# Paged attention in steps of four pages, keys and values fetched apart, and the prompt bias added by TensorE

## The chip, the cores and the metric

One NeuronCore of a Trainium2 chip runs the whole program. The metric is the device time of one execution in microseconds. Three runs of the kernel before took 2260.86, 2262.31 and 2270.95 us; the median is 2262.31 us.

## What is computed

One inference step of a decoder with two layers, for a prompt of 512 tokens and for eight samples of four tokens each that share the weights. Each layer projects the residual stream into four head groups: a short gated convolution (A), gated DeltaNet (B), HGRN2 (C) and differential attention with a relative bias (D). Their outputs are concatenated and projected back, followed by a layer norm, a channel mixer (a SwiGLU in layer 0, eight experts in layer 1) and another layer norm. The change is in group D alone:

```python
def _diff_attn_core(q, k, v, q_pos, k_pos, lam, rel_bias):
    s = jnp.einsum('bqhmd,bkhmd->bmhqk', q, k) * (HEAD_DIM_DQK ** -0.5)
    bias = jnp.transpose(rel_bias[_t5_bucket(q_pos, k_pos)], (2, 0, 1))
    s = jnp.where(k_pos[None, :] <= q_pos[:, None], s + bias, -jnp.inf)
    p = jax.nn.softmax(s, axis=-1)
    w = p[:, 0] - lam * p[:, 1]
    return jnp.einsum('bhqk,bkhv->bqhv', w, v)
```

There are 4 heads, each with two maps (m) of width 32 and values of width 64. The prompt attends to itself in blocks of 128 queries. Each sample attends to 2048 past positions, held in 16 pages of 128 positions that a page table names, and to its own four new tokens.

## The kernel before

All engines are programmed through a framework that takes the instructions in program order, finds their dependences tile by tile, and plans each engine's queue ahead of time from estimated durations: an instruction earlier in the program has priority when it is ready in the plan, and later ones fill what is left. On the chip every engine then works through its own queue in that fixed order. So the instructions of one stage lie between those of others.

`mixers` (line 477) holds the four head groups of a layer. In program order it runs `d_in` (the projections of D), `mix_b`, `d_attn`, `mix_a`, `mix_c` and the gates. `mix_b` has a long serial chain of small VectorE work with four round trips through DRAM; the attention of D and the projections of A and C (the tile `st`, split in three fp32r products of 128 by 128 weights) fill around it.

`d_sample` (line 596) does the samples in two groups g of four samples b. A step j takes one page of each of the four samples. `page` (line 607) reads page numbers into registers of SyncE, eight at a time, and issues one fetch of 256 KB for each page: 128 partitions of 2 KB, of which the first half is the transposed keys and the second half the values. The buffer `kv` has KVB = 9 slots of 2 KB a partition, shared with the exponentials of the prompt heads. Then, for each step:

- eight products of the queries `qs` with the keys: 32 columns of weights, 128 moving columns, sample b writing PSUM partitions 32b to 32b + 31. The loop is over the two tiles tl outside and over b inside (line 626). In the trace this is `dx<-kv,qs`.
- reduce_max on VectorE (L632), exp on ScalarE (L634), one transposition on TensorE (L635), its copy by VectorE (L637).
- four products with the values, 256 moving columns (`dx<-kv,et`), and `select` (lines 600 to 603), which keeps each row's own head with a multiplication and a reduction on VectorE.

16 steps, and one for the new tokens, make a group; then the 17 partial results are weighted and added (lines 658 to 674).

`d_head` (line 676) is one block of 128 queries of one prompt head, 16 in a layer. For both maps it multiplies queries and keys over nk = 128 to 512 positions (`dx<-arr,y`), adds the bias of the last 256 positions on VectorE in PSUM (L691), takes the maximum (L692) and the exponential (L694). VectorE then scales the second map (L699) and joins the two (L700); TensorE transposes the result into a third PSUM tile (L703) and multiplies by the values. `d_attn` runs a head after every second step.

An fp32 product is two passes on TensorE, and the trace has two records for it; a product of fp32r operands, and a transposition, is one.

Of the kernel before, what the change touches and what calls it, by code (L numbers as in the profile page):

```python
# [18 lines left out]
L = 2  # L19
# [20 lines left out]
KVB = 9  # L40
# [146 lines left out]
def _pack(a):  # L187
# [19 lines left out]
    f["kv"] = _cols(np.concatenate([kp, a["cache_v"].reshape(L, npool, 128, 256)], 3))  # L207
# [58 lines left out]
def _body(ctx, tc, I, O):  # L266
# [210 lines left out]
    def mixers(l, y32, hook):  # L477
# [110 lines left out]
        def d_attn(q, k, vt, qs):  # L588
            heads = [d_head(q, k, vt, qb, tl, h2) for qb in range(4) for tl in range(2) for h2 in range(2)]
            for n, _ in enumerate(d_sample(k, vt, qs)):  # L590
                if n % 2 == 1:
                    heads[n // 2]()
            for i in range(2):
                rms_d(y32[:, 6:8], i, nd[:, l:l + 1])

        def d_sample(k, vt, qs):
            od = y32[:, 6:8]
            ends = []

            def select(pj, po):  # L600
# [4 lines left out]
            regs = []  # L605

            def page(i):
                if i == len(regs):
                    with ExitStack() as qx:
                        if len(ends) > 8:  # L610
                            qx.enter_context(tc.issue_after(ends[-9].ins))
                        _, r = nc.values_load_multi_w_load_instructions(ptb[:, i:i + 8], engines=[mybir.EngineType.SP],
                                                                        min_val=0, max_val=I["kv"].shape[1] - 1)
                    regs.extend(r)
                t = dq.tile([128, 512], F32, name="kv", bufs=KVB)
                ends.append(SP.dma_start(t, I["kv"][l][bass.ds(regs[i], 1)].rearrange("o p f -> p (o f)")))
                return t

            for g in range(2):
                nm = dq.tile([128, 20], F32, name="nm", bufs=2)  # L620
                zz = dq.tile([128, 20], F32, name="zz", bufs=2)
                pj = dq.tile([128, 17, 64], F32, name="pj", bufs=1)
                for j in range(16):
                    kv = [page(64 * g + 4 * j + b) for b in range(4)]
# [5 lines left out]
                    if j == 15:  # L630
                        tt(V, ps[:, 0:128], ps[:, 0:128], bs[:, 0:128], OP.add)
                    V.reduce_max(nm[:, j:j + 1], ps[:, 0:128], axis=AX.X, negate=True)  # L632
                    e = dq.tile([128, 128], F32, name="e", bufs=3)
                    S.activation(e, ps[:, 0:128], AF.Exp, bias=nm[:, j:j + 1], accum_out=zz[:, j:j + 1])  # L634
                    PE.transpose(ps[:, 128:256], e, ident)  # L635
                    et = dq.tile([128, 128], F32, name="et", bufs=3)
                    V.tensor_copy(et, ps[:, 128:256])  # L637
                    for b in range(4):
                        mm(ps[32 * b:32 * b + 32, 256:512], et[:, 32 * b:32 * b + 32], kv[b][:, 256:512])
                    select(pj[:, j], ps[:, 256:512])  # L640
# [6 lines left out]
                V.reduce_max(nm[:, 16:17], ps[:, 0:32], axis=AX.X, negate=True)  # L647
                sn = dq.tile([128, 32], F32, name="sn", bufs=1)
                S.activation(sn, ps[:, 0:32], AF.Exp, bias=nm[:, 16:17], accum_out=zz[:, 16:17])
                pe = dx()  # L650
                PE.transpose(pe[0:32, 0:128], sn, ident)
                etn = dq.tile([32, 128], F32, name="etn", bufs=1)
                V.tensor_copy(etn, pe[0:32, 0:128])
                po = dx()
                for b in range(4):
                    mm(po[32 * b:32 * b + 32, 0:256], etn[:, 32 * b:32 * b + 32], vt[0:32, 4, :])
                select(pj[:, 16], po[:, 0:256])
                V.tensor_reduce(nm[:, 17:18], nm[:, 0:17], axis=AX.X, op=OP.min)
                wj = dq.tile([128, 17], F32, name="wj", bufs=1)
                S.activation(wj, nm[:, 0:17], AF.Exp, bias=nm[:, 17:18], scale=-1.0)  # L660
                tt(V, zz[:, 0:17], zz[:, 0:17], wj, OP.mult)
                V.tensor_reduce(zz[:, 17:18], zz[:, 0:17], axis=AX.X, op=OP.add)
                V.reciprocal(zz[:, 17:18], zz[:, 17:18])
                V.tensor_scalar(zz[:, 18:19], C("m1"), neglam[:, l:l + 1], 1.0, op0=OP.mult, op1=OP.add)
                V.tensor_scalar(zz[:, 19:20], C("m1"), -1.0, zz[:, 18:19], op0=OP.mult, op1=OP.add)
                tt(V, zz[:, 17:18], zz[:, 17:18], zz[:, 19:20], OP.mult)
# [3 lines left out]
                V.tensor_scalar(rd, rd, zz[:, 17:18], None, op0=OP.mult)  # L670
# [3 lines left out]
                V.tensor_copy(od[:, :, NP_ + 16 * g:NP_ + 16 * g + 16], pf[:, 0:32].rearrange("p (a t) -> p a t", a=2))  # L674

        def d_head(q, k, vt, qb, tl, h2):
# [7 lines left out]
            def go():  # L684
                zz = dq.tile([128, 8], F32, name="zp", bufs=2)
                e, pss = [], []
                for m in range(2):
                    p0 = h2 * 64 + m * 32
                    ps = dx()
                    mm(ps[:, 0:nk], q[p0:p0 + 32, tl, q0:q0 + 128], k[p0:p0 + 32, tl, 0:nk])  # L690
                    tt(V, ps[:, b0:nk], ps[:, b0:nk], bt[:, h, 256 - (nk - b0):256], OP.add)  # L691
# [13 lines left out]
                po = pss[0]  # L705
# [1386 lines left out]
```

## Time and profile before

| | |
|---|---|
| median of three runs | 2262.31 us |
| span of the profiled execution, first to last instruction | 2255.7 us |
| median less that span | 6.6 us |
| PE busy in the span | 2093.5 us (93%) |
| VectorE busy | 1495.0 us (66%) |
| ScalarE busy | 820.8 us (36%) |
| mean granted TensorE clock | 0.953 of 2.4 GHz |
| page fetches | 256, 256 KB each |

The profiled execution's own time is its span and what lies around it; only its span was recorded, and the median of the runs lies 6.6 us above that. The attention runs from 84 to 447 us in layer 0 and from about 1044 to 1442 us in layer 1. PE is TensorE's matmul queue, DVE is VectorE, ACT is ScalarE, SPq is SyncE's queue, which issues nearly all DMAs. In a row such as `dx<-kv,qs 128*32 128x128 f32` the names are the tile written and the tiles read, 128*32 the weights (rows by columns) and 128x128 the moving operand. A busy time is the union of the records' lengths; the lengths contain the way through the array, so a matmul's own cost is better read from the distance between starts.

### The profile page before, as it was taken

What the parts mean: (1) busy time and instruction counts of PE and PEld (TensorE: products, weight loads), DVE (VectorE), ACT (ScalarE), POOL (GpSimd) and SP (SyncE); (2) the same over time, 40 slices, a digit from 0 to 9 for tenths busy, and PEclk for the clock granted to TensorE, in tenths of its full rate; (3) what the DMA queues carried; (4) which work ended last, traced back from release to release, by engine and by line L of the source; (5) the groups of instructions that cost most, each with busy time, mean ns of one, the idle gap of its engine ahead of it and who ended that gap; (6) DMA issues with size and microseconds to landing.
All of it is one profiled execution on the core that took longest, in us unless ns stands there. A gap on an engine that the chain in (4) does not pass through costs nothing.

```text
span 2255.7 us, 47059 instructions
## 1 busy us (share of the span) xinstructions
PE 2093.5 (93%) x18052; PEld 1843.4 (82%) x18052; DVE 1495.0 (66%) x2944; ACT 820.8 (36%) x1842; POOL 431.1 (19%) x544
## 2 busy tenths in 40 slices
PE   8999899998999999999999999897999998898986
PEld 7976676778999999889777666686889897897875
DVE  4675657767333334746756667568989987777795
ACT  3522425455222223435323345444334433334221
POOL 0100002102000000111000111003514436535431
PEclk9998999989999999999988999798999999999998
DMA  6343434242222323542524343237868786586751
GB/s 235 99 137 119 124 114 142 86 134 94 93 78 84 98 90 103 169 155 90 160 90 129 123 132 96 93 104 243 257 216 284 223 286 203 171 269 206 276 182 60
DMA packets 153490, 340.92 MB, mean 151 GB/s; under 512 B 29411, under 2 KB 39784, under 8 KB 153256
## 3 DMA queue, kind: packets, MB, share of 16 engines
q1 hardware_dynamic: 140840, 324.09, 45.1%
q0 software_dynamic: 3312, 11.60, 1.6%
q10 hardware_dynamic: 9104, 2.13, 0.5%
q8 instruction: 144, 2.36, 0.5%
q14 instruction: 90, 0.74, 0.1%
HBM read 319.91 MB, written 17.85 MB: 150 GB/s over the span
## 4 chain that ended last, share of the span: by engine, by line
PE 66%; DVE 12%; POOL 7%; issue 5%; ACT 4%; DMA 4%; SPq 0%; DVEq 0%; ACTq 0%; POOLq 0%
PE st L290 32%; PE ff L290 12%; PE mx L290 9%; PE dx L290 8%; DVE wl L293 4%; POOL m_g L293 2%; DVE wh L366 2%; PE ee L290 2%; POOL m_u L293 2%; ACT wh L368 1%; POOL hg L293 1%; POOL r L1402 1%; ACT ev L1668 1%; DMA ys_d<-yt 1%; DMA sd<-d 1%
## 5 line engine op out<-in xcount | busy, mean ns | idle before, releaser
L293 DVE TENSOR_TENSOR wl<-wraw,wh 128x1024 fp32r<-128x1024 f32 (+2 forms) x474 | 562.7, 1196 | 283.7 <-ACT wh L368 260.8
L290 PE MATMUL st<-xh,wh 128*128 128x256 f32 (+1 forms) x1536 | 465.0, 303 | 15.5 <-ACT wh L368 11.2
L290 PE MATMUL st<-xl,wh 128*128 128x256 f32 (+1 forms) x1536 | 463.0, 301 | 6.6 <-DVE xl L293 6.5
L290 PE MATMUL st<-xh,wl 128*128 128x256 f32 (+1 forms) x1536 | 462.3, 301 | 1.8 <-DVE wl L293 1.8
L368 ACT ACTIVATE wh<-wraw 128x1024 fp32r<-128x1024 f32 (+2 forms) x280 | 274.1, 980 | 496.3 <-PE st L290 290.1
L290 PEld LDWEIGHTS st<-xh,wh 128*128 128x128 f32 x1536 | 297.7, 194 | 34.2 <-issue 13.1
L290 PEld LDWEIGHTS st<-xh,wl 128*128 128x128 f32 x1536 | 297.8, 194 | 25.6 <-issue 21.4
L290 PEld LDWEIGHTS st<-xl,wh 128*128 128x128 f32 x1536 | 298.2, 194 | 24.8 <-issue 13.9
L290 PE MATMUL st<-xg,wh 128*128 128x416 f32 (+4 forms) x880 | 248.7, 358 | 29.8 <-ACT ev L1668 27.4
L290 PE MATMUL st<-xg,wl 128*128 128x208 f32 (+4 forms) x880 | 215.0, 245 | 3.6 <-DVE wl L293 3.3
L290 PEld LDWEIGHTS st<-xg,wh 128*128 128x128 f32 x880 | 167.1, 190 | 38.9 <-ACT ev L1668 35.7
L290 PEld LDWEIGHTS st<-xg,wl 128*128 128x128 f32 x880 | 169.8, 193 | 8.3 <-DVE wl L293 8.2
L366 DVE CAST wh<-wraw 128x1024 fp32r<-128x1024 f32 (+2 forms) x194 | 159.2, 821 | 16.5 <-PE ee L290 12.1
L290 PE MATMUL st<-hg,wh 128*128 128x416 f32 (+4 forms) x440 | 126.9, 367 | 2.2 <-POOL hg L293 2.2
L1402 POOL TENSOR_SCALAR r<-r,par 128x256 f32<-128x256 f32 (+1 forms) x32 | 29.0, 920 | 487.1 <-ACT xh L1401 487.1
L290 PE MATMUL st<-hg,wl 128*128 128x208 f32 (+4 forms) x440 | 110.0, 250 | 1.6 <-DVE wl L293 1.5
L290 PE MATMUL ff<-hh,wl 128*128 128x256 f32 (+1 forms) x352 | 103.3, 293 | 3.2 <-DVE wl L293 3.2
L290 PE MATMUL st<-wh,xg 128*128 128x256 f32 x528 | 104.1, 291 | 0.0
L290 PE MATMUL ff<-hh,wh 128*128 128x256 f32 (+1 forms) x352 | 103.2, 293 | 1.0 <-ACT wh L368 1.0
L290 PE MATMUL ff<-hl,wh 128*128 128x256 f32 (+1 forms) x352 | 102.1, 290 | 0.0
L290 PE MATMUL ff<-xh,wl 128*128 128x256 f32 (+1 forms) x352 | 101.8, 289 | 0.0
L290 PE MATMUL ff<-xl,wh 128*128 128x256 f32 (+1 forms) x352 | 101.7, 289 | 0.0
(566 smaller groups left out, 4296.8 us busy)
## 6 DMA issues: line engine op xcount, KB each, us to landing
kv<-in_kv_dram SPq DMA_DIRECT2D x256, 256.0 KB, 3.7
wraw<-in_w_in_dram SPq DMA_DIRECT2D x57, 512.0 KB, 4.1
wraw<-in_m_g_dram SPq DMA_DIRECT2D x54, 512.0 KB, 4.5
wraw<-in_m_u_dram SPq DMA_DIRECT2D x54, 512.0 KB, 4.5
wraw<-in_m_g_dram SPq DMA_DIRECT2D x65, 256.0 KB, 4.4
wraw<-in_m_u_dram SPq DMA_DIRECT2D x65, 256.0 KB, 4.7
wraw<-in_w_o_dram SPq DMA_DIRECT2D x32, 512.0 KB, 3.6
wraw<-in_m_d_dram SPq DMA_DIRECT2D x40, 384.0 KB, 3.6
```

The source lines that it names most:

```text
L290: return PE.matmul(out, lhsT, rhs, start=start, stop=stop)
L293: return e.tensor_tensor(out, a, b, op=op)
L366: V.tensor_copy(h, r)
L368: S.activation(h, r, AF.Copy)
L1402: G.tensor_scalar(ri[:, u], ri[:, u], gcol[:, u:u + 1], bcol[:, u:u + 1], op0=OP.mult, op1=OP.add)
L1668: S.activation(t[:, 0:2 * cap], ps[:, 0:2 * cap], AF.Copy)
```

## The change

`page` goes. Keys and values are separate inputs, `kc` and `vc`, and each page is fetched in two transfers of 128 KB (128 partitions of 1 KB). `pages` fetches two pages of each of four samples into four tiles `pg` of two pages, from PGB = 7 slots of 2 KB a partition; `kv` keeps KVB = 5 slots. A step takes four pages of each sample: two units u of two pages for the keys, then one maximum, one exponential, four transpositions, one copy of 512 columns, now on ScalarE, then two units for the values, accumulated in PSUM, and one `select`. There are 4 steps and one for the new tokens in a group; `d_sample` yields twice a step, and the 16 heads are spread over 20 yields. In the key products the loop over b is outside and the loop over tl inside, with 256 moving columns.

In `d_head` the bias is added by a product of the identity with the bias rows into the same PSUM accumulation, the second map is scaled by ScalarE, and the transpositions go into the second of the two PSUM tiles instead of a third. The diff, without the packing of inputs and the renumbered columns:

```diff
-KVB = 9
+KVB = 5
+PGB = 7
...
+            done = 0
             for n, _ in enumerate(d_sample(k, vt, qs)):
-                if n % 2 == 1:
-                    heads[n // 2]()
+                while done < 16 and done < (n + 1) * 16 / 20:
+                    heads[done]()
+                    done += 1
...
+            def indices(i):
+                out = []
+                for o in (0, 8):
+                    with ExitStack() as qx:
+                        if len(ends) > PGB:
+                            qx.enter_context(tc.issue_after(ends[-PGB - 1].ins))
...
+            def pages(src, regs, u):
+                out = []
+                for b in range(4):
+                    t = dq.tile([128, 2, 256], F32, name="pg", bufs=PGB)
+                    for a in range(2):
+                        ends.append(SP.dma_start(t[:, a], I[src][l][bass.ds(regs[4 * (2 * u + a) + b], 1)].rearrange("o p f -> p (o f)")))
+                    out.append(t)
+                return out
...
+                def soft(ps, j, n):
+                    V.reduce_max(nm[:, j:j + 1], ps[:, 0:n], axis=AX.X, negate=True)
+                    e = big("e", n)
+                    S.activation(e, ps[:, 0:n], AF.Exp, bias=nm[:, j:j + 1], accum_out=zz[:, j:j + 1])
+                    return e
...
+                for j in range(4):
+                    regs = indices(64 * g + 16 * j)
                     ps = dx()
-                    for tl in range(2):
-                        for b in range(4):
-                            mm(ps[32 * b:32 * b + 32, 0:128], qs[:, tl, 4 * g + b, :], kv[b][:, 128 * tl:128 * tl + 128],
-                               start=tl == 0, stop=tl == 1)
...
+                    for u in range(2):
+                        for b, t in enumerate(pages("kc", regs, u)):
+                            for tl in range(2):
+                                mm(ps[32 * b:32 * b + 32, 256 * u:256 * u + 256], qs[:, tl, 4 * g + b, :],
+                                   t[:, :, 128 * tl:128 * tl + 128], start=tl == 0, stop=tl == 1)
+                    if j == 3:
+                        tt(V, ps[:, 384:512], ps[:, 384:512], bs[:, 0:128], OP.add)
+                    e = soft(ps, j, 512)
+                    yield
+                    for a in range(4):
+                        PE.transpose(ps[:, 128 * a:128 * a + 128], e[:, 128 * a:128 * a + 128], ident)
+                    et = big("et", 512)
+                    S.activation(et, ps, AF.Copy)
+                    for u in range(2):
+                        vs = pages("vc", regs, u)
+                        for a in range(2):
+                            for b in range(4):
+                                o = 128 * (2 * u + a) + 32 * b
+                                mm(ps[32 * b:32 * b + 32, 0:256], et[:, o:o + 32], vs[b][:, a], start=2 * u + a == 0, stop=2 * u + a == 3)
+                    select(pj[:, j], ps[:, 0:256])
                     yield
...
-                    mm(ps[:, 0:nk], q[p0:p0 + 32, tl, q0:q0 + 128], k[p0:p0 + 32, tl, 0:nk])
-                    tt(V, ps[:, b0:nk], ps[:, b0:nk], bt[:, h, 256 - (nk - b0):256], OP.add)
+                    mm(ps[:, 0:nk], q[p0:p0 + 32, tl, q0:q0 + 128], k[p0:p0 + 32, tl, 0:nk], stop=False)
+                    mm(ps[:, b0:nk], ident, bt[:, h, 256 - (nk - b0):256], start=False)
...
-                V.tensor_scalar(e[1][:, 0:nk], e[1][:, 0:nk], zz[:, 5:6], None, op0=OP.mult)
+                S.activation(e[1][:, 0:nk], e[1][:, 0:nk], AF.Copy, scale=zz[:, 5:6])
...
-                pw = dx()
+                po, pw = pss
```

## Rows read from the trace of the kernel before

**Rows 1.** Windows by stage; the columns are named in the first row.

```profile
core 0: us, PE busy (x) PEld busy (x) DVE busy (x) ACT busy (x) POOL busy (x), PEclk, DMA share, GB/s
...
80.00:485.00 405.00, 386.30 (x4128) 286.19 (x4127) 272.11 (x744) 163.41 (x446) 43.15 (x89) 0.93 0.37 117
...
1036.00:1450.00 414.00, 391.96 (x4132) 292.39 (x4132) 276.46 (x752) 163.89 (x447) 45.62 (x89) 0.93 0.38 115
```

**Rows 2.** Chain of waits, shares by line, of 80:485 and 1036:1450.

```profile
by line: PE st L290 27.2%; PE mx L290 24.6%; PE dx L290 23.2%; DMA wk<-te 2.7%; issue 2.6%; DVE wl L293 1.4%; PE dx L703 1.4%; PE dx L635 1.4%; DMA kv<-in_kv_dram 1.0%; DMA sd<-d 1.0%; DVE kq L293 0.8%; ACT row L527 0.7%; DVE rd L669 0.5%; 
...
by line: PE mx L290 25.4%; PE st L290 24.7%; PE dx L290 22.0%; DMA sd<-d 2.3%; issue 2.0%; DMA bk<-sd 2.0%; POOL ex L293 1.8%; DMA kv<-in_kv_dram 1.5%; PE dx L635 1.3%; PE dx L703 1.2%; DMA out_gs_dram<-lt 0.7%; POOL di L293 0.7%; DVE r L29
```

**Rows 3.** Timeline of PE at 144: start, length, count, idle time.

```profile
145.26 0.30 PE L290 MATMUL st<-xh,wl 128*128 128x288 f32 x1
145.39 0.29 PE L290 MATMUL st<-xh,wh 128*128 128x288 f32 x1
145.62 0.41 PE L290 MATMUL dx<-kv,qs 128*32 128x128 f32 x2
145.95 0.40 PE L290 MATMUL st<-xl,wh 128*128 128x288 f32 x1
146.19 0.27 PE L635 MATMUL dx<-cst,e 128*128 128x128 f32 x1
```

**Rows 4.** Timeline of PE at 148 and at 84.

```profile
147.72 0.64 PE L290 MATMUL dx<-kv,et 128*32 128x256 f32 x8
148.18 0.62 PE L290 MATMUL dx<-kv,qs 128*32 128x128 f32 x10
148.73 0.40 PE L290 MATMUL st<-xh,wl 128*128 128x288 f32 x1
...
84.09 1.08 PE L290 MATMUL dx<-kv,qs 128*32 128x128 f32 x32
85.10 0.48 PE L290 MATMUL dx<-arr,y 32*128 32x128 f32 x2
```

**Rows 5.** Groups of PE by shape in 80:485: count, busy us, mean ns.

```profile
L290 PE MATMUL dx<-kv,qs 128*32 128x128 f32 x512 | 47.4, 292 | 0.0
L290 PE MATMUL mx<-kq 64*32 64x32 f32 x720 | 26.2, 196 | 0.0
L290 PE MATMUL dx<-kv,et 128*32 128x256 f32 x256 | 23.0, 406 | 0.3 <-DVE et L637 0.3
...
L290 PE MATMUL mx<-wk 32*32 32x32 f32 x480 | 7.3, 203 | 4.6 <-issue 2.8 <-DVE wk L897 1.8
```

**Rows 6.** Timeline of PE at 104: products with full 128 by 128 weights.

```profile
104.34 0.71 PE L290 MATMUL mx<-cst,w 128*128 128x128 f32 x4
104.81 0.38 PE L290 MATMUL st<-xh,wh 128*128 128x288 f32 x1
```

**Rows 7.** Groups of VectorE by shape in 80:485.

```profile
L603 DVE TENSOR_REDUCE pj<-r 128x64 f32<-128x256 f32 x34 | 20.3, 597 | 0.1
L293 DVE TENSOR_TENSOR r<-dx,cst 128x256 f32<-128x256 f32 x34 | 14.2, 419 | 11.9 <-PE dx L290 11.6
...
L293 DVE TENSOR_TENSOR dx<-dx,bt 128x256 f32<-128x256 f32 x24 | 10.3, 429 | 11.2 <-PE dx L290 11.1
...
L637 DVE COPY et<-dx 128x128 f32<-128x128 f32 x32 | 9.0, 285 | 7.6 <-PE dx L635 7.2
...
L669 DVE TENSOR_REDUCE rd<-pj 128x64 f32<-128x1088 f32 x2 | 4.1, 2047 | 0.0
```

**Rows 8.** Page buffers: fetches, time to landing, two waits on the chain.

```profile
L616 SPq DMA_DIRECT2D kv<-in_kv_dram x256: 332/333/1752, 31.2 to 1386.5; - x128
...
DMA to landing us min/median/max: 2.6/3.7/7.8
...
239.69 4.09 DMA kv<-in_kv_dram
...
1146.12 6.41 DMA kv<-in_kv_dram
```

More of the change, by code (lines that the diff above doesn't have):

```diff
@@ L206, in _pack @@
     kp = a["cache_k"].reshape(L, npool, 128, 2, 128).transpose(0, 1, 4, 3, 2).reshape(L, npool, 128, 256)
-    f["kv"] = _cols(np.concatenate([kp, a["cache_v"].reshape(L, npool, 128, 256)], 3))
+    f["kc"] = _cols(kp)
+    f["vc"] = _cols(a["cache_v"].reshape(L, npool, 128, 256))
     f["pt"] = _cols(a["page_table"].reshape(2, 4, 16).transpose(0, 2, 1).reshape(1, NB * NPG))
@@ L589, in d_attn @@
             heads = [d_head(q, k, vt, qb, tl, h2) for qb in range(4) for tl in range(2) for h2 in range(2)]
+            done = 0
             for n, _ in enumerate(d_sample(k, vt, qs)):
-                if n % 2 == 1:
-                    heads[n // 2]()
+                while done < 16 and done < (n + 1) * 16 / 20:
+                    heads[done]()
+                    done += 1
+            while done < 16:
+                heads[done]()
+                done += 1
             for i in range(2):
@@ L598, in d_sample, with big @@
             ends = []
+            def big(name, n):
+                return dq.tile([128, 512], F32, name="kv", bufs=KVB)[:, 0:n]
             def select(pj, po):
@@ L603, in select @@
                 V.tensor_reduce(pj, r4.rearrange("p h v -> p v h"), axis=AX.X, op=OP.add)
-            regs = []
-            def page(i):
-                if i == len(regs):
+            def indices(i):
+                out = []
+                for o in (0, 8):
                     with ExitStack() as qx:
[L610 to L617, printed above, removed]
@@ L619, in d_sample @@
-            for g in range(2):
[L620 to L624, printed above, removed]
-                    ps = dx()
-                    for tl in range(2):
-                        for b in range(4):
-                            mm(ps[32 * b:32 * b + 32, 0:128], qs[:, tl, 4 * g + b, :], kv[b][:, 128 * tl:128 * tl + 128],
-                               start=tl == 0, stop=tl == 1)
[L630 to L640, printed above, removed]
@@ new lines, in indices @@
+                        if len(ends) > PGB:
+                            qx.enter_context(tc.issue_after(ends[-PGB - 1].ins))
+                        _, r = nc.values_load_multi_w_load_instructions(ptb[:, i + o:i + o + 8], engines=[mybir.EngineType.SP],
+                                                                        min_val=0, max_val=I["kc"].shape[1] - 1)
+                    out.extend(r)
+                return out
[6 more added lines that the diff above has]
+                    out.append(t)
+                return out
@@ new lines, in d_sample @@
+            for g in range(2):
+                nm = dq.tile([128, 8], F32, name="nm", bufs=2)
+                zz = dq.tile([128, 10], F32, name="zz", bufs=2)
+                pj = dq.tile([128, 5, 64], F32, name="pj", bufs=2)
+                def soft(ps, j, n):
[5 more added lines that the diff above has]
+                    regs = indices(64 * g + 16 * j)
+                    ps = dx()
+                    for u in range(2):
[18 more added lines that the diff above has]
+                    select(pj[:, j], ps[:, 0:256])
@@ L646, in d_sample @@
                 tt(V, ps[:, 0:32], ps[:, 0:32], bs[:, 128 + 32 * g:160 + 32 * g], OP.add)
[L647 to L651, printed above, removed]
+                sn = soft(ps, 4, 32)
+                PE.transpose(ps[0:32, 0:128], sn, ident)
@@ L652, in d_sample @@
                 etn = dq.tile([32, 128], F32, name="etn", bufs=1)
-                V.tensor_copy(etn, pe[0:32, 0:128])
-                po = dx()
+                V.tensor_copy(etn, ps[0:32, 0:128])
                 for b in range(4):
[L656 to L666, printed above, removed]
+                    mm(ps[32 * b:32 * b + 32, 0:256], etn[:, 32 * b:32 * b + 32], vt[0:32, 4, :])
@@ new lines, in d_sample @@
+                select(pj[:, 4], ps[:, 0:256])
+                yield
+                V.tensor_reduce(nm[:, 5:6], nm[:, 0:5], axis=AX.X, op=OP.min)
+                wj = dq.tile([128, 5], F32, name="wj", bufs=1)
+                S.activation(wj, nm[:, 0:5], AF.Exp, bias=nm[:, 5:6], scale=-1.0)
+                tt(V, zz[:, 0:5], zz[:, 0:5], wj, OP.mult)
+                V.tensor_reduce(zz[:, 5:6], zz[:, 0:5], axis=AX.X, op=OP.add)
+                V.reciprocal(zz[:, 5:6], zz[:, 5:6])
+                V.tensor_scalar(zz[:, 6:7], C("m1"), neglam[:, l:l + 1], 1.0, op0=OP.mult, op1=OP.add)
@@ L667, in d_sample @@
+                V.tensor_scalar(zz[:, 7:8], C("m1"), -1.0, zz[:, 6:7], op0=OP.mult, op1=OP.add)
+                tt(V, zz[:, 5:6], zz[:, 5:6], zz[:, 7:8], OP.mult)
                 tt(V, pj, pj, bc(wj, 64), OP.mult)
@@ L669, in d_sample @@
                 V.tensor_reduce(rd, pj.rearrange("p j v -> p v j"), axis=AX.X, op=OP.add)
-                V.tensor_scalar(rd, rd, zz[:, 17:18], None, op0=OP.mult)
+                V.tensor_scalar(rd, rd, zz[:, 5:6], None, op0=OP.mult)
                 pf = dx()
@@ L674, in d_sample @@
                 V.tensor_copy(od[:, :, NP_ + 16 * g:NP_ + 16 * g + 16], pf[:, 0:32].rearrange("p (a t) -> p a t", a=2))
+                yield
         def d_head(q, k, vt, qb, tl, h2):
@@ L704, in go @@
                 S.activation(e[1][:, 0:nk], pw[:, 0:nk], AF.Copy)
-                po = pss[0]
                 for kb in range(qb + 1):
```

## The prediction

> **What bounds the kernel now.** I read the page first (PE busy 93% of the span), then cut the span into stages, because only two of them change: the mixers of layer 0 from 80 to 485 us and of layer 1 from 1036 to 1450 us. There PE is busy 386.3 of 405 us and 392.0 of 414 us, VectorE 272.1 and 276.5, ScalarE some 163, and the DMA engines 0.37 of the time [rows 1]. The chain of waits says the same from the other side: the five PE lines of `st`, `mx` and `dx` make 77.8% of it in layer 0 (27.2 + 24.6 + 23.2 + 1.4 + 1.4) and 74.6% in layer 1; DMA pieces and issue make about 7%, and some 15% is left for VectorE, ScalarE and GpSimd together [rows 2]. So a microsecond of PE in these stages counts for about 0.76, and one of VectorE for little. The reader is to see also that "busy" is not "streaming". A key product that stands alone between `st` products takes from 145.39 to 146.19 us, in which two `st` products of 0.13 us ran as well: 0.54 us for it, though its two records start 0.13 us apart, and the `st` product behind it needs 0.24 instead of 0.13 us [rows 3]. Handled in one go, four whole steps of key products (32 records) take from 84.09 to 85.10 us, 0.25 us a step [rows 4]. The price of the sample attention on PE is thus set by how it is cut into groups and in which order a group runs.
>
> **The change part by part.** All terms are for both layers.
>
> *Key products.* Their 512 records of layer 0 are busy 47.4 us [rows 5]; the timeline has 101 groups of them in 32 steps, the first at 84.09 us [rows 4] and the last at 430 us, about three a step, since a step's pages land one after the other and the plan issues each product when its page is there. With 0.11 us for each return to `st` that is 58.5 us a layer, 3.66 us for two steps. The new unit u of two pages has the same number of columns in half the records. But b is now the outer loop: the two products of one sample stand together and write the same 32 columns of the array. Two rows price that: `mx<-kq`, whose loop writes one place several times running, is busy 26.2 us for 720 records, 36 ns each; `mx<-wk`, which goes to another place with each product, 7.3 for 480, 15 ns, both with 32 moving columns [rows 5]. A tile that lands alone is four passes of 256 columns in one place: 0.22 us each (eight records of 256 in two rounds take 0.46 from 147.72 to 148.18 [rows 4]), and 0.30 for the change of shape and back, 1.18 us. Four alone are 4.7 us; with one pair landed together (three slots of 0.44 instead of four) 4.0; all four landed, five slots, 2.5; wholly side by side, as at 84, 1.2. I take 4.0, near the groups before, where about half of the lone products had merged: 32 x (4.0 - 3.66) = +11 us, with the ends -79 and +33.
>
> The Trainium skill, "TensorEngine Tiling (Array Packing)", Key Properties, says that changing the tiling mode drains the engine and that tiles work independently. The first half agrees with the 0.54 us of row 145.62. By the second half alone a unit would cost the 1.2 us whatever the order, and the key products would fall by 79 us; the pair `mx<-kq` and `mx<-wk` speaks against that, and it is the low end of rival one.
>
> *Value products.* 23.0 us busy and 34 groups a layer now [rows 5], 26.7 us with the returns, 3.3 us for four steps. After: the first unit of values has mostly landed while the maximum, exponential, transposition and copy run, and goes in one group (0.30 + 4 x 0.22 = 1.2 us). The eighth value tile needs the slot of the first, which only the first unit's products free, with 3.7 us to landing behind that [rows 8]; so the second unit goes in two groups, 0.74 + 1.18. Sum 3.1, for 16 steps -3 us; ends: all in one group 2.1 (-20 us), every tile alone 6.8 (+56 us).
>
> *Bias on PE.* 48 products of 256 columns and 16 of 128, fp32 with the full 128 by 128 identity. Four such records of 128 columns run from 104.34 to 104.81 us [rows 6]: 0.235 us for a product of 128 columns, 0.47 for 256. 48 x 0.47 + 16 x 0.235 = +26 us. It stands where PE is busy 95%, so nothing hides it; the low end is 0, if it fell wholly into idle time of PE.
>
> *Transpositions.* 64 before and after, of the same shape: nothing.
>
> PE in all: 26 + 11 - 3 = +34 us, on the chain at 0.76: +26 us.
>
> *VectorE.* Selects fall from 68 to 20 (48 x (0.597 + 0.419) = 49 us), the copy to `et` goes (64 x 0.285 = 18), the bias additions go (48 x 0.43 and 16 shorter, about 25), 32 scalings go (near the bias row, 0.43 each, 14), the final weighting shrinks to 5/17 (about 6) [rows 7]: some 110 of 549 us, a fifth. ScalarE takes 16 copies of 512 columns and the scalings, and loses 48 exponentials; it has room at 40%. If the 15% of the chain that is not PE, DMA or issue, 123 us in 819, shrank by that fifth, the gain were 25 us; where it shrinks, PE work queued behind steps in, and the other end is 0. I take -12 us.
>
> *Fetches.* 512 instead of 256, each half as large, 0.333 us of SyncE's queue and its register work [rows 8]; a tile now waits for two. SyncE is in order, and behind a page that waits for its slot stand the weight loads of `st` and the round trips' neighbours; PE in turn is in order behind a late page. Before, two such waits on the chain are 4.09 and 6.41 us [rows 8]. The ring of seven lets fewer bytes wait ready than a step needs (sixteen tiles). I take +3 us, ends -10 (both waits gone) and +20 (twice more of each).
>
> The Trainium skill, "DMA: Bandwidth & Descriptors", in its table of before and after trn3, gives 2 KiB a partition as the least transfer that saturates the DMAs of the generations before; the halved pages have 1 KB. No row of this kernel has such a fetch, and with the engines at 0.37 the rule touches the time to landing alone.
>
> Sum: 26 - 12 + 3 = +17 us. Against the profiled execution's span of 2255.7 us that is 2272.7; the median of the runs lies 6.6 us above that span, so the forecast is 2279 us, 0.8% slower. About 0.5% (11 us) is what a measurement of this kernel tells from no change.
>
> **Rivals.** *One, faster: the key tiles come in bulk.* If the plan holds the key products back behind the heads' work until all four tiles of a unit have landed, a unit costs 2.5 us: 32 x (2.5 - 3.66) = -37, the values in one group -20, the bias +26: -31 on PE, -24 on the chain, with -12 for VectorE -36 us: 2226 us. It turns faster than before once a unit costs under 3.4 us, all else as forecast. For it: KVB + PGB is 12 slots instead of 9, and fewer groups. Against it: 101 groups in 32 steps show that the plan takes a page as soon as it lands.
>
> *Two, no change.* VectorE's relief returns what PE adds: the serial chain of `mix_b` runs on VectorE, and a fifth less work beside it may give the whole 25 us: 26 - 25 = +1, 2263 us. Against it: DMA round trips and PE, not VectorE, are the large pieces of the chain.
>
> *Three, much slower.* Keys and values both come tile by tile: +33, +56 and +26 on PE are 115, on the chain 87, with +3 and -12: 2340 us. For it speaks the ring of seven, against it the time that the softmax gives the values to land; a half of it, 2310, is likelier than the whole.
>
> **How the numbers follow.** The forecast 0.43 (its own range 2266 to 2300: slower 0.37, same 0.06), rival one 0.26 (faster 0.24, same 0.02), rival two 0.20 (same 0.14, faster 0.04, slower 0.02), rival three 0.11 (slower). That makes faster 0.28, same 0.22, slower 0.50. The range reaches from 2228, near rival one's price, to 2318, past half of rival three: 2228 to 2318.
>
> **What would show it.** In the changed profile the PE busy time of the two mixer stages would grow by some 30 us; a new row of identity products of 128x256 near 0.4 us a pair of records; groups of four `qs` records of 256 columns, about 0.22 us apart, standing alone between `st` products, 50 or so a layer. VectorE's busy time falls by about 110 us while the stages don't shorten. I am wrong if the `qs` records come in groups of 16 whose starts lie within a few ns of each other, if the stages shorten although PE's work grew, or if PE's idle time, 19 and 22 us now, is what changed most.

## The result and the profile after

The changed kernel takes 2276.3 us (median of 10 runs, 2268 to 2287) against 2264.1 us for the kernel before on the same chip: the ratio is 1.0058, 95% interval 1.0034 to 1.0083. It is slower by 0.6%, where 0.8% was forecast. The direction and the size were right; the account behind them was right in some terms and wrong in others that cancelled, so the nearness of the two numbers is in part luck.

The windows of the two mixer stages after the change, from shortly before the attention to the end of the mixers (columns as in [rows 1]; layer 1 as a whole now starts some 11 us later):

```profile
core 0: us, PE busy (x) PEld busy (x) DVE busy (x) ACT busy (x) POOL busy (x), PEclk, DMA share, GB/s
80.00:492.00 412.00, 396.85 (x3932) 285.71 (x3930) 225.28 (x591) 167.61 (x422) 44.46 (x89) 0.97 0.41 118
1050.00:1471.00 421.00, 401.72 (x3929) 290.33 (x3928) 229.86 (x601) 167.83 (x422) 47.41 (x89) 0.94 0.40 117
```

PE is busy 399 us on average instead of 389 [rows 1], VectorE 228 instead of 274, and both stages are longer (by 17 us together, against the windows of the account below). The granted clock rose, from 0.93 [rows 1] to 0.97 and 0.94: that was not forecast. The records of PE by shape in layer 0 (count, busy us, mean ns), which answer to [rows 5]:

```profile
L292 PE MATMUL dx<-pg,qs 128*32 128x256 f32 x256 | 51.9, 385 | 0.0
...
L292 PE MATMUL dx<-pg,kv 128*32 128x256 f32 x256 | 31.6, 417 | 1.2 <-ACT kv L661 1.2
...
L292 PE MATMUL dx<-bt,cst 128*128 128x256 f32 x48 | 16.5, 425 | 0.0
...
L292 PE MATMUL dx<-bt,cst 128*128 128x128 f32 x16 | 3.9, 326 | 0.0
```

The same products on the timeline of PE (start, length, count), which answers to [rows 3, 4, 6]:

```profile
134.21 1.05 PE L292 MATMUL dx<-pg,qs 128*32 128x256 f32 x4
135.19 0.49 PE L292 MATMUL dx<-bt,cst 128*128 128x128 f32 x2
135.44 0.38 PE L292 MATMUL st<-xh,wl 128*128 128x288 f32 x1
135.65 0.29 PE L292 MATMUL st<-xh,wh 128*128 128x288 f32 x1
...
141.31 1.48 PE L292 MATMUL dx<-pg,kv 128*32 128x256 f32 x18
143.06 0.33 PE L729 MATMUL dx<-cst,kv 128*128 128x128 f32 x1 [0.26 <-DVE kv L726]
143.32 0.63 PE L292 MATMUL dx<-pg,kv 128*32 128x256 f32 x4
143.87 0.40 PE L292 MATMUL st<-xl,wh 128*128 128x288 f32 x1
...
145.24 0.49 PE L292 MATMUL dx<-bt,cst 128*128 128x128 f32 x2
145.49 0.38 PE L292 MATMUL st<-xl,wh 128*128 128x288 f32 x1
...
147.55 1.05 PE L292 MATMUL dx<-pg,kv 128*32 128x256 f32 x10
148.53 0.40 PE L292 MATMUL st<-xh,wh 128*128 128x288 f32 x1
```

At 134.21 the keys of one sample (four records) hold PE for 0.98 us. At 141.31 a step's first unit of values goes together with one tile of the second, 18 records in 1.49 us; the other tiles follow at 143.32 (0.55 us) and 147.55 (0.98 us). At 145.24 the bias of a 128-column block takes 0.25 us to the next start.

VectorE's `select` answers to [rows 7]: 34 of each became 10.

```profile
L613 DVE TENSOR_REDUCE pj<-r 128x64 f32<-128x256 f32 x10 | 5.9, 591 | 0.1
...
L295 DVE TENSOR_TENSOR r<-dx,cst 128x256 f32<-128x256 f32 x10 | 4.2, 423 | 1.5 <-PE dx L292 1.3
```

On the whole page VectorE's busy time fell from 1495.0 to 1403.1 us. The page's list of fetches (count, KB each, us to landing), which answers to [rows 8]:

```profile
pg<-in_kc_dram SPq DMA_DIRECT2D x256, 128.0 KB, 2.5
pg<-in_vc_dram SPq DMA_DIRECT2D x256, 128.0 KB, 2.3
```

The half pages land in 2.5 and 2.3 us where the whole ones took 3.7 [rows 8]. The Trainium skill, "DMA: Bandwidth & Descriptors", in its table of before and after trn3, wants 2 KiB a partition to saturate the DMAs; at 1 KB the queue's share of the engines' time rose only from 45.1 to 45.7% for 36,864 more packets, so the rule decides nothing here. The chain of waits of layer 1 by line, and its page waits:

```profile
by line: PE dx L292 27.0%; PE st L292 26.2%; PE mx L292 21.7%; issue 2.8%; POOL ex L295 2.0%; DMA sd<-d 2.0%; SPq L621 1.8%; DMA pg<-in_kc_dram 1.8%; PE dx L729 1.1%; DMA pg<-in_vc_dram 1.1%; SPq L631 1.1%; POOL di L295 0.9%; PE dx L659 0.6
...
1087.43 4.55 DMA pg<-in_vc_dram
...
1227.15 3.98 DMA pg<-in_kc_dram
...
1258.43 3.51 DMA pg<-in_kc_dram
```

Three page waits of 12.0 us and SyncE's lines L621 and L631 (2.9% of 421 us, 12 us) stand on this chain; layer 0's has none in its list. Before, the two layers had 4.1 and 6.4 us of page waits [rows 8].

**An account by kind.** Busy times count the way through the array twice where records overlap. For each PE record I took the distance from its start to the start of the next, less the idle time ahead of the next, and summed by the tile that is written and read. The windows of after are the two above; those of before are these:

```profile
80.00:484.00 404.00, 385.30 (x4119) 285.19 (x4118) 271.11 (x741) 163.41 (x446) 43.15 (x89) 0.93 0.37 117
1038.00:1450.00 412.00, 389.96 (x4117) 290.39 (x4116) 274.46 (x749) 163.69 (x446) 45.62 (x89) 0.92 0.38 116
```

For the two windows together, in us, with the stage clock of layer 0 and layer 1 ("all PE" and "idle" add up to the windows):

| kernel | keys | values | bias | `st` | `mx` | all PE | idle | clock |
|---|---|---|---|---|---|---|---|---|
| before | 80.8 | 38.8 | - | 304.4 | 239.2 | 775.3 | 40.7 | 0.93, 0.92 |
| after | 91.8 | 58.9 | 31.7 | 286.9 | 227.7 | 798.5 | 34.4 | 0.97, 0.94 |

Keys +11, values +20 and bias +32 are 63 us; `st` and `mx` give back 29, transpositions and the small products of D about 11, and PE's idle time 6. The stages grow by 17 us, the span by 22. The edges of a window cut the stream of `st` products at other places in each kernel (1878 to 1925 of their records, up to 7 us apart), so differences of a few us in `st` and "all PE" mean nothing.

Counting neighbouring records of one kind as a group: 94 and 90 groups of key products before, 50 and 43 after, 34 and 26 of them four records alone, where the prediction looked for 50 or so a layer. The values keep 34 groups a layer, but before 26 and 25 of them were whole steps of eight records, since a page's values had come with its keys; after, 29 of 68 are two or four records.

### The profile page after: what moved, and what is told of

The parts are those of the page before. It is cut to its first block, busy times and chain, and to the rows that moved or that the text cites. A ratio compares the mean times of both kernels' runs of the same rounds, so it can differ in the third digit from the quotient of the medians.

```text
span 2277.6 us, 46766 instructions
## 1 busy us (share of the span) xinstructions
PE 2123.2 (93%) x17668; PEld 1850.6 (81%) x17668; DVE 1403.1 (62%) x2640; ACT 829.8 (36%) x1794; POOL 436.8 (19%) x544
## 3 DMA queue, kind: packets, MB, share of 16 engines
q1 hardware_dynamic: 177704, 324.11, 45.7%
## 4 chain that ended last, share of the span: by engine, by line
PE 67%; DVE 10%; POOL 7%; ACT 5%; issue 5%; DMA 4%; SPq 1%; ACTq 0%; DVEq 0%; POOLq 0%
PE st L292 32%; PE ff L292 12%; PE dx L292 10%; PE mx L292 9%; DVE wl L295 3%; POOL m_g L295 2%; PE ee L292 2%; DVE wh L368 2%; POOL m_u L295 2%; ACT wh L370 1%; POOL r L1427 1%; POOL hg L295 1%; DMA sd<-d 1%; ACT ev L1693 1%; POOL ex L295 1%
## 5 line engine op out<-in xcount | busy, mean ns | idle before, releaser
L292 PE MATMUL st<-xl,wh 128*128 128x256 f32 (+1 forms) x1536 | 458.3, 298 | 5.5 <-DVE xl L295 5.4
L292 PE MATMUL st<-xh,wl 128*128 128x256 f32 (+1 forms) x1536 | 457.5, 299 | 3.2 <-DVE wl L295 3.2
```

Of the source, the lines that this page charges most:

```text
L292: return PE.matmul(out, lhsT, rhs, start=start, stop=stop)
```

## The experiments

Twelve kernels ran, each timed in five rounds against the kernel before on its chip; there the kernel before had medians of 2271.0 (e1 to e4), 2269.3 (e5 to e8) and 2267.3 us (e9 to e12). Differences to before are therefore taken from the ratios, times 2264 us, and differences "to after" from the differences of the ratios. The account by kind of each (as above) is in this table, with the stage clock and the mean granted clock of the timed executions that the ratio uses. Each profile is of one execution, which can lie well off the median: that of e5 took 2229.7 us, its shortest, against a median of 2248.8, and that of e11 was its longest.

| run | keys | values | bias | all PE | idle | stage clock | clock of executions | ratio to before |
|---|---|---|---|---|---|---|---|---|
| e1 | 94.5 | 55.2 | - | 769.5 | 46.4 | 0.95, 0.94 | 0.952 | 0.9960 (0.9931 to 0.9988) |
| e2 | 70.3 | 52.0 | 31.8 | 774.3 | 34.1 | 0.95, 0.96 | 0.956 | 0.9967 (0.9940 to 0.9994) |
| e3 | 79.1 | 37.7 | 27.7 | 797.1 | 32.0 | 0.93, 0.93 | 0.944 | 1.0082 (1.0054 to 1.0109) |
| e4 | 97.5 | 57.0 | 31.6 | 813.8 | 39.4 | 0.97, 0.92 | 0.950 | 1.0163 (1.0116 to 1.0209) |
| e5 | 41.9 | 55.5 | 32.5 | 741.1 | 48.9 | 0.94, 0.94 | 0.949 | 0.9906 (0.9873 to 0.9939) |
| e6 | 40.0 | 41.8 | - | 745.3 | 66.6 | 0.88, 0.86 | 0.933 | 0.9893 (0.9852 to 0.9934) |
| e7 | 45.0 | 37.9 | - | 706.3 | 68.8 | 0.92, 0.89 | 0.941 | 0.9801 (0.9765 to 0.9836) |
| e8 | 47.9 | 54.4 | 33.1 | 749.6 | 49.5 | 0.94, 0.94 | 0.950 | 0.9923 (0.9893 to 0.9953) |
| e9 | 75.8 | 41.8 | - | 781.8 | 38.3 | 0.90, 0.94 | 0.944 | 1.0011 (0.9984 to 1.0039) |
| e10 | 92.1 | 38.5 | 31.1 | 783.3 | 42.8 | 0.95, 0.94 | 0.954 | 1.0026 (0.9998 to 1.0053) |
| e11 | 39.6 | 57.5 | 31.1 | 763.5 | 34.8 | 0.92, 0.92 | 0.954 | 0.9821 (0.9787 to 0.9855) |
| e12 | 45.8 | 43.5 | - | 732.4 | 55.6 | 0.86, 0.89 | 0.937 | 0.9795 (0.9760 to 0.9829) |

**e1: the changed kernel, bias on VectorE again.**

```diff
-mm(ps[:, 0:nk], q[...], k[...], stop=False)
-mm(ps[:, b0:nk], ident, bt[:, h, 256 - (nk - b0):256], start=False)
+mm(ps[:, 0:nk], q[...], k[...])
+tt(V, ps[:, b0:nk], ps[:, b0:nk], bt[:, h, 256 - (nk - b0):256], OP.add)
```

> The changed kernel with the bias of the prompt heads back on VectorE. Theory one (PE's work in the mixer stages passes to the end at about 0.76): PE's own time falls by the 32 us that the bias products take in the changed trace (14.4 and 17.3 us from start to start), VectorE gets 25 us back, of which a tenth counts: 24 - 3 = 21 us less than the changed kernel, about 2255 us, 0.5% under the kernel before (2264). Rival (VectorE's serial chain or the plan's placing sets the end, PE's extra work only fills holes): no gain, 2276 us or a few us more.

2260.2 us, 22 us less than after. PE's work falls by 29 us and its idle time rises by 12, less than the 25 us that the additions take on VectorE.

**e2: the changed kernel, key products with tl outside and b inside.**

```diff
-for b, t in enumerate(pages("kc", regs, u)):
-    for tl in range(2):
+ks = pages("kc", regs, u)
+for tl in range(2):
+    for b in range(4):
```

> The changed kernel with the key products' loops turned round: tl outside, b inside, as in the kernel before. Theory one, with the price of a group set by which part of the array its products write: a lone tile costs 0.74 instead of 1.18 us and the last group of a unit 1.18; the keys fall from about 105 to 86 us over both layers, times 0.76 is 14 us: 2262 us. Rival (products of different samples run side by side whatever their order): nothing changes in the lone groups but their number rises, 2276 to 2285 us.

2259.5 us, 21 us less than after; the keys fall by 21.5 us. A sample that lands alone now sends one product, and the second products go together when the last sample is there. On its timeline of PE:

```profile
129.60 0.62 PE L292 MATMUL dx<-pg,qs 128*32 128x256 f32 x2
...
137.02 1.05 PE L292 MATMUL dx<-pg,qs 128*32 128x256 f32 x10
138.00 0.40 PE L292 MATMUL st<-xh,wh 128*128 128x288 f32 x1
```

48 groups have two records (0.55 us to the next start), 21 ten records (0.98 us).

**e3: the kernel before, with only the bias on TensorE** (the edit of e1, backwards, in the kernel before).

```diff
-mm(ps[:, 0:nk], q[...], k[...])
-tt(V, ps[:, b0:nk], ps[:, b0:nk], bt[:, h, 256 - (nk - b0):256], OP.add)
+mm(ps[:, 0:nk], q[...], k[...], stop=False)
+mm(ps[:, b0:nk], ident, bt[:, h, 256 - (nk - b0):256], start=False)
```

> The kernel before with only the bias on PE. Theory one: 64 products of 0.235 to 0.47 us, 26 to 32 us of PE, times 0.76, less 3 us for VectorE's 25: 19 us more than before, 2283 us. Rival (hidden in PE's idle time of 41 us in the two stages, VectorE relieved): within 5 us of before, or under it.

2285.8 us, 19 us more than before, with 27.7 us of bias on PE. Together with e1 the term stands: about 20 us of time.

**e4: the changed kernel, the scaling of the second map on VectorE again.**

```diff
-S.activation(e[1][:, 0:nk], e[1][:, 0:nk], AF.Copy, scale=zz[:, 5:6])
+V.tensor_scalar(e[1][:, 0:nk], e[1][:, 0:nk], zz[:, 5:6], None, op0=OP.mult)
```

> The changed kernel with the scaling of the second map back on VectorE. Theory one: 14 us of VectorE's time moved, of which a tenth counts, and as much off ScalarE: within 5 us of the changed kernel, 2276 us. Rival (VectorE sets the end): 10 us or more slower, 2286 us.

2302.5 us, 24 us more than after. Theory one missed, and the rival seemed to hold. But its windows don't show a VectorE that sets the end:

```profile
80.00:500.00 420.00, 400.53 (x3941) 291.68 (x3940) 232.90 (x608) 159.66 (x405) 43.79 (x89) 0.97 0.41 116
1058.00:1491.00 433.00, 413.06 (x3927) 295.50 (x3926) 237.19 (x615) 158.84 (x406) 46.76 (x89) 0.92 0.39 113
```

VectorE is busy 7 to 8 us more a stage, with nearly half its time free. Of the account's 20 us, 15 are PE work of the same products (keys +6, `st` +7 among them) and 5 are idle time. The runs e9, e11 and e12 take this up.

**e5: the changed kernel, tl outside and the samples from 3 to 0**, so that the first product of a unit waits for its last page and the unit goes in bulk.

```diff
+for tl in range(2):
+    for b in (3, 2, 1, 0):
```

> The changed kernel with tl outside and b inside from 3 down to 0, so that the first key product of a unit waits for the tile that lands last and the rest of the unit follows in one group. Theory one: 32 units of about 1.2 us (eight rounds of 0.11 us side by side and 0.3 us for the change of shape) instead of 3.2, 62 us less PE, times 0.76: 47 us less than the changed kernel, about 2229 us. Rival (the arrival of the pages or the softmax chain sets the pace of the attention, and PE's shorter groups only leave holes): 2270 to 2285 us, since the keys now wait longer.

2248.8 us, 34 us less than after; the keys cost 41.9 instead of 91.8 us, as expected, but PE's idle time rises by 14 and the time falls by less than the 47 us expected. A whole unit, sixteen records, now takes as long as one sample alone did at 134.21 in the changed kernel:

```profile
136.95 1.07 PE L292 MATMUL dx<-pg,qs 128*32 128x256 f32 x16
137.95 0.39 PE L292 MATMUL st<-xl,wh 128*128 128x256 f32 x1
```

**e8: the changed kernel's own loop, b outside, but from 3 to 0.**

```diff
-for b, t in enumerate(pages("kc", regs, u)):
+for b, t in reversed(list(enumerate(pages("kc", regs, u)))):
     for tl in range(2):
```

> The changed kernel with b outside from 3 down to 0 and tl inside: the units go in one group as in the run with tl outside, but the two products of a sample stand together. Theory one (products that write the same 32 columns run one after the other and hold up those behind them): a unit costs 2.5 us in five slots, 20 us less PE than the changed kernel, 2261 us, some 30 us more than with tl outside. Rival (side by side whatever the order): the same as with tl outside, about 2229 us, and groups of 16 records in 1.2 us.

The prediction held that the two products of a sample, standing together, run in one place one after the other, so that four landed tiles cost five slots, 2.5 us. The row of the timeline says otherwise:

```profile
137.55 1.09 PE L292 MATMUL dx<-pg,qs 128*32 128x256 f32 x16
138.57 0.49 PE L292 MATMUL dx<-bt,cst 128*128 128x128 f32 x2
```

Sixteen records take 1.02 us here too, and the first records of its four samples start within 40 ns of each other, though in the queue the four records of a sample stand together. The Trainium skill, "TensorEngine Tiling (Array Packing)", Key Properties, says that tiles work independently; the prediction weighed this against `mx<-kq` and `mx<-wk` [rows 5], and the run agrees with the rule. In time, e8 (0.9923) and e5 (0.9906) can't be told apart.

**e6: the kernel before, with only its key loop from 3 to 0.**

```diff
-for b in range(4):
+for b in (3, 2, 1, 0):
```

> The kernel before with one edit: in the key products b runs from 3 down to 0. Theory one: 64 steps in groups of eight products at about 0.75 us instead of 1.83, 65 us or more less PE, times 0.76: about 50 us under the kernel before, 2214 us. Rival (pace of the pages and the softmax): the same as before or slower, 2264 to 2275 us.

2248.6 us, 24 us less than before. PE's key work halves (80.8 to 40.0), but half of the 50 us that were expected is missing. The windows of its profile show what stood against it:

```profile
80.00:480.00 400.00, 370.61 (x4131) 286.00 (x4130) 272.91 (x745) 164.06 (x447) 41.61 (x89) 0.88 0.40 119
1034.00:1446.00 412.00, 374.77 (x4137) 289.70 (x4137) 276.72 (x753) 163.87 (x447) 43.85 (x89) 0.86 0.39 117
```

The idle time (window less PE busy) is 67 us instead of 41, and the clock is 0.88 and 0.86 instead of 0.93 and 0.92; all of PE's work falls by 30 us, though the keys fall by 41. These windows are only 4 us shorter than those of before and can't be set against the medians' 24: the profiled execution of before is one of its faster ones (clock 0.953, where its executions beside these runs have 0.946 on average), that of e6 an ordinary one (0.931 against 0.933).

**e10: the changed kernel, only the value products from 3 to 0.**

```diff
 for a in range(2):
-    for b in range(4):
+    for b in (3, 2, 1, 0):
```

> The changed kernel, only with the value products' loop over the samples run 3 to 0, so that the first of a group waits for the last page of the unit. Theory one (value products cost 29 us a layer because pages land one at a time, and of the 20 us that they grew by nearly all goes): values at 18 to 21 us a layer on PE, 18 us less in both layers, 2262 us. Rival (the second unit waits for its slots as a whole, so holding back the first product turns the saving into idle time of PE): PE's idle time up by 10 us or more in all and the time within 6 us of the changed kernel.

The values fall from 58.9 to 38.5 us, the price of before, and the two units of a step go in one group each:

```profile
143.49 1.07 PE L292 MATMUL dx<-pg,kv 128*32 128x256 f32 x16 [1.75 <-ACT kv L661]
144.49 0.40 PE L292 MATMUL st<-xl,wh 128*128 128x288 f32 x1
...
148.45 1.07 PE L292 MATMUL dx<-pg,kv 128*32 128x256 f32 x16
149.45 0.40 PE L292 MATMUL st<-xl,wh 128*128 128x288 f32 x1
```

The time falls to 1.0026, 7 us less than after, where the intervals overlap. Both theories are half right: the 20 us on PE are real, 8 us come back as idle time and the clock is lower. The 1.75 us before 143.49 end with ScalarE's copy, so that unit had landed by then.

**e7: the changed kernel with the edits of e5, e1 and e10.**

```diff
+for b in (3, 2, 1, 0):   # keys, inside tl
+for b in (3, 2, 1, 0):   # values
+tt(V, ps[:, b0:nk], ps[:, b0:nk], bt[:, h, 256 - (nk - b0):256], OP.add)
```

> The changed kernel with tl outside and b from 3 down to 0 for the keys, b from 3 down to 0 for the values, and the bias back on VectorE. Theory one: keys 62 us, values about 25 us (groups of 16 records at 1.2 us or of 8 at 0.75 instead of 4.1 us a step) and bias 32 us less PE, times 0.76, less 3 us for VectorE: about 87 us under the changed kernel, 2190 us. Rival (pace of the pages and the softmax): no better than the run with the keys alone, and the values' wait makes it slower: 2230 us or more.

2228.1 us, 2.0% below before and 58 us below after, where 87 were expected. PE's work falls by 92 us; idle time takes back 34:

```profile
80.00:458.00 378.00, 346.03 (x3863) 271.59 (x3861) 231.92 (x622) 164.88 (x421) 47.52 (x89) 0.92 0.46 129
1015.00:1412.00 397.00, 360.20 (x3860) 276.17 (x3858) 233.98 (x629) 167.49 (x421) 43.59 (x89) 0.89 0.44 124
```

**e9, e11, e12: the scaling once more.** e9 is the kernel before with the scaling on ScalarE; e11 is e5, and e12 is e7, with it on VectorE.

```diff
 e9
-V.tensor_scalar(e[1][:, 0:nk], e[1][:, 0:nk], zz[:, 5:6], None, op0=OP.mult)
+S.activation(e[1][:, 0:nk], e[1][:, 0:nk], AF.Copy, scale=zz[:, 5:6])
 e11, e12
-S.activation(e[1][:, 0:nk], e[1][:, 0:nk], AF.Copy, scale=zz[:, 5:6])
+V.tensor_scalar(e[1][:, 0:nk], e[1][:, 0:nk], zz[:, 5:6], None, op0=OP.mult)
```

> The kernel before, only with the scaling of a head's second map on ScalarE. Theory one (moving it is worth in itself what putting it back cost in the changed kernel, some 24 us, since VectorE's queue releases the heads late): 2240 us, and PE's idle time in the two mixer stages, 18.7 and 22.0 us, falls or the order's PE sum falls. Rival (the 24 us were the plan's: another arrangement of the queues, not a wait on VectorE): within 6 us of before, or slower.

> The changed kernel with the key products held back to the last page (samples 3 to 0, tiles outside) and the scaling of a head's second map on VectorE. Theory one (the scaling on VectorE releases heads late and costs 20 us or more wherever it stands): 2270 us or more against 2249 with the scaling on ScalarE. Rival (its price in the changed kernel was the plan's): within 6 us of 2249.

> The changed kernel with keys and values held back to the last page, the bias on VectorE, and now the scaling of a head's second map on VectorE too, so that the heads stand as before the change. Theory one (20 us or more for the scaling on VectorE): 2248 us or more against 2228. Rival (the plan's): within 6 us of 2228.

e9 takes 2267.1 us, the same as before. e11 takes 2229.6 us, 19 us *less* than e5; e12 takes 2224.1 us, the same as e7. So VectorE instead of ScalarE costs +24, -19 and about 0 us in three kernels, and the move the other way is worth nothing in the fourth. The instruction has no fixed price here. Every queue is planned anew when a duration changes; which choice of the plan makes the two large differences was not found, and that stays open. Part of both goes with the granted clock: e4 has 0.950 where after has 0.960, and e11 0.954 where e5 has 0.949. It also sets the limit for the other runs: a time difference of 20 us alone proves no term of the sum, so the verdicts above rest on the account of PE first. e12, e7 and e11 are the fastest of all, and their intervals overlap.

## Why the prediction came out right

**Key products: +11 forecast; +11.0 measured in their own records, about +1 with the returns.** The forecast's prices hold the slower `st` product behind each group, while the account counts it under `st`. The groups fell from 184 to 93, at the 0.11 us of [rows 3] each some 10 us, so like for like the term is, as an estimate, +1. With the returns a unit costs 3.2 us instead of 4.0 (91.8 us and 93 returns over 32 units), and two old steps 3.2 instead of 3.66 (80.8 us and 184 returns). The old price was built from busy times [rows 5], which hold the way through the array. In the new one the number of groups was right, three a unit, and a lone tile's 1.18 us was near: 0.98 us and 0.11 for the return. What was wrong is the price of two tiles that land together: "three slots", 1.6 us, where the eight records of such a group take 0.99 us to the next start. The "five slots" of the b-outer order are refuted by e8. What the groups show is simpler: at the full clock, and to the next start, a group takes 0.12 us and 0.43 us for each 256-column product *in its fullest place*. Two records take 0.55 us, eight in four places 0.57, four in one place 0.98, eight with two products in each of two places 0.99, sixteen in four places 1.00 to 1.02, eighteen with three products in one place 1.41 to 1.49. So b outside costs only because tiles land, and are issued, one at a time: four lone samples are 4 x 0.98, and with tl outside 3 x 0.55 + 0.98. That is e2.

**Value products: -3 forecast, +20 measured.** This is the step that failed: "The first unit of values has mostly landed ... and goes in one group", three groups a step, against a price of before that was too high. With 68 returns, 7.5 us, on either side as in the forecast, the values of before cost 46 us, not 53.4; that is 7 of the 23 us missed, again busy time taken for cost. The other 16 us are after the change, 66 us instead of 50, and go with the groups: 34 a layer and not 24. The step at 141.31 goes just as forecast, in three groups (1.49 + 0.55 + 0.98 = 3.0 us against 3.1), but not all do. The trace of before held the reason: values that come with their keys are there, whole, once the softmax is done. Fetching them apart gave that up; e10 gets the whole groups back by order alone, and whether more slots would keep the saving in time was not tried.

**Bias: +26 forecast, +32 and +28 (e3) measured** on PE. It was right that nothing hides it; e1 and e3 give about 20 us of time.

**What the forecast lacked: `st` and `mx` cost 29 us less after, about 19 without the returns.** Their products are the same: over the whole span, where no window cuts them, the 12,800 records cost 25 us less. Two things can be put beside it. The groups of key and value products fell from 252 to 161, all of it keys, and at 0.11 us for each return that is 10 us, which belongs to the key term. And the granted clock rose. In the trace of before, a stretch of layer 0 shows one loss of it (windows, columns as in [rows 1]):

```profile
172.00:176.00 4.00, 2.93 (x149) 2.24 (x150) 1.01 (x4) 0.00 (x0) 0.00 (x0) 1.00 0.77 283
176.00:180.00 4.00, 2.30 (x67) 1.81 (x67) 1.23 (x4) 0.46 (x2) 0.00 (x0) 0.54 0.03 8
180.00:184.00 4.00, 4.00 (x26) 2.25 (x25) 1.14 (x3) 1.66 (x5) 0.00 (x0) 0.50 0.00 0
192.00:196.00 4.00, 4.00 (x26) 3.66 (x25) 2.86 (x6) 0.00 (x0) 0.87 (x1) 0.50 0.00 0
196.00:200.00 4.00, 4.00 (x39) 3.19 (x38) 2.34 (x6) 0.00 (x0) 0.26 (x1) 0.90 0.48 112
```

From 172 to 180 us PE is busy 2.93 and 2.30 of 4 us. Then the clock stands at 0.50, the lower level of 1.2 GHz, until some 196 us, although PE is busy all the time again. The changed kernel has no such gap there and keeps 2.4 GHz:

```profile
172.00:176.00 4.00, 4.00 (x136) 2.48 (x136) 1.99 (x4) 0.68 (x2) 0.00 (x0) 1.00 0.23 74
176.00:180.00 4.00, 4.00 (x130) 2.82 (x122) 1.99 (x6) 1.85 (x5) 0.00 (x0) 1.00 0.22 65
```

But such a gap is neither needed nor enough. In the kernel before, 2.7 us without PE work from 1088 to 1096 us left the clock at 1.00, and from 328 us it stands at 0.50 though PE had been busy all the time:

```profile
1088.00:1092.00 4.00, 3.25 (x30) 2.52 (x23) 2.71 (x8) 0.62 (x4) 0.00 (x0) 1.00 0.84 238
1092.00:1096.00 4.00, 2.07 (x16) 1.75 (x14) 2.15 (x13) 0.25 (x1) 0.00 (x0) 1.00 1.02 360
1096.00:1100.00 4.00, 4.00 (x27) 2.88 (x26) 3.25 (x11) 1.07 (x2) 2.13 (x4) 1.00 0.41 93
...
324.00:328.00 4.00, 4.00 (x51) 3.80 (x50) 0.79 (x2) 0.00 (x0) 0.00 (x0) 0.81 0.07 28
328.00:332.00 4.00, 4.00 (x21) 2.12 (x21) 1.30 (x3) 0.00 (x0) 0.00 (x0) 0.50 0.00 0
```

With the stage clock at 0.955 instead of 0.925, 544 us of `st` and `mx` would shorten by 17 us. That sum, 27 with the returns, is near the 29 measured; the shares are worked out and were not tried apart.

**The clock of whole executions.** All executions of the kernel before have the same queues. Still, over 69 of those timed beside e1 to e12 (within 1.5% of the fastest on their chip), the mean granted clock runs from 0.937 to 0.957 and the time from 2287 to 2249 us; a line through them falls by 16 us for each 0.01 of clock. It does not tell whether the clock sets the time or waits move both. Their average clock is 0.946; the ten executions of the changed kernel have 0.956 to 0.964, 0.960 on average. As an estimate, if the 16 us held between kernels too, which no run tests, the changed kernel got some 23 us back from a higher clock, and without that it would be about 35 us slower than before instead of 12. The forecast has no such term: that is the luck in its number. The same estimate covers much of what is missing or odd elsewhere. e6 has 0.933, some 21 us, which with its 24 makes 45 of the 50 expected; e7 has 0.941 against 0.960, some 31 us, which with its 58 makes 89 where 87 were expected; and of e4's 24 us some 16 go with the clock, of e11's 19 some 8.

**From PE to time: 0.76.** e1, e2 and e3 change PE's work by -29, -24 and +22 us and the time by -22, -21 and +19: 0.77, 0.85 and 0.85. Less comes through in e5 (34 of 57), e8 (31 of 49), e7 (58 of 92) and e10 (7 of 15), where PE's idle time grows by 8 to 34 us and the clock is lower than in the changed kernel. All these ratios set medians against the account of one execution, and are rough.

**VectorE: -12 forecast.** Its busy time fell by 92 us, near the forecast 110, and PE's idle time by 6. Rival two, in which VectorE returns 25 us, did not come. **Fetches: +3 forecast.** On the chains they went from 10.5 to some 24 us, within the term's ends but at the upper one; no run takes this apart.

So +34 us on PE were forecast and +23 came, as 63 less 40, and the sum of 17 us stood against 17 in the stages, 22 in the span and 12 between the medians. Rival one, the keys in bulk, was not what the plan did; e5 shows that it was there to be had, at 1.3 us a unit before the return, if the last page's product comes first. Two figures of the prediction are off by its own terms: half of rival three is 2301 us and not 2310, and with the +3 us of the fetches rival one turns faster than before under 3.3 us a unit, not 3.4. The measured 3.2 lies under both and the kernel is slower all the same, since the old price was 3.2 too and the values cost more.

## What to carry to other kernels

Price products on parts of the array by the fullest part of a group, from start to start, and not by busy time. If pages land one at a time and the engine takes its work in order, put the product that needs the last page first; here that is worth 1.1% in the kernel before and 1.4 to 1.5% in the changed one, with one loop changed. Before you split a fetch, look at what the other half did by coming early; and before you believe a 1% difference, make the same edit in a second arrangement of the queues, and compare the granted clocks.

## What was not expected of the hardware

The clock's price: two windows with 2.8 us without PE work in 8 us, and then about 20 us at half the clock with PE always busy, while nearly as long a gap elsewhere left the clock as it was. And the clock differs between executions of one kernel: with it, the time of the kernel before ranges over 38 us. Of the 28 stages of the fourteen profiles, the five with 29 us of idle time or more had 0.86 to 0.92, the 23 with 27 us or less 0.89 to 0.97, so idle time is not all that counts. But saved PE work that leaves PE waiting can be paid for twice: in e6 and e7 more idle time and a lower clock stood beside the saving.
